# Moving the conditioning loads to GpSimd's queue and the last GpSimd subtractions to VectorE in a two-layer encoder kernel

## The chip, the cores and the metric

The kernel runs on one core of one Trainium2 chip. The metric is the device time of one execution in microseconds. A measurement is the median over runs; the profile is one further execution of the same program, taken by the hardware profiler.

The engines are named as the profile names them: PE is TensorE (PEld its weight load), DVE is VectorE, ACT is ScalarE, POOL is GpSimd and SP is SyncE. A name with a q behind it (ACTq, POOLq, SPq) is the instruction queue of that engine where it issues a DMA or waits.

## The reference, cut to what matters

Two layers work on x of 256 tokens by 1024 features. Six vectors per layer come from a conditioning input c.

```python
cond = jax.nn.silu(c)
for l in range(DEPTH):
    ada = cond @ w_ada[l] + b_ada[l]
    sh1, sc1, g1, sh2, sc2, g2 = jnp.split(ada, 6)
    u = x * (1.0 + sc1) + sh1
    mix = hybrid_mixer(u, ...)
    x = layer_norm(ALPHA * x + g1 * mix, ln_g[l, 0], ln_b[l, 0])
    u = x * (1.0 + sc2) + sh2
    ffn = peer_ffn(u, peer_wq[l], peer_keys[l], peer_u[l], peer_v[l])
    x = layer_norm(ALPHA * x + g2 * ffn, ln_g[l, 1], ln_b[l, 1])
```

`hybrid_mixer` holds two attentions, a long convolution, three gates and an output product. `peer_ffn` makes queries, picks experts by two rounds of top 16, and multiplies with all 16384 rows of `peer_u` and of `peer_v`.

## The kernel before, in words

**Products in split precision.** Every large product is made of three matmuls in a 32-bit matmul format: a weight tile (128 partitions by 1024 elements) is split into a high part, which ACT writes (line 86), and a low part, raw minus high, which DVE or POOL writes (line 88). The activations have a high and a low part too: `uh` and `ul` hold u transposed. PE then adds high by high, high by low and low by high.

**The weight stream.** `Stream` loads the weight tiles one after the other on SP's queue (line 67) into three raw buffers, and splits up to two tiles ahead of the product that wants them. A flag per tile says whether DVE ("v") or POOL ("g") writes its low part. POOL has the first eight tiles of layer 0, the query tiles and the first 24 tiles of `peer_u` of each layer.

**Order of work.** The order is written out by hand. Each engine runs its own instructions in the order in which the program lists them, and waits for the others by semaphores. Small work is put between the products by generators that are advanced one step at a time (`Background.pump`).

**The conditioning.** `w_ada` comes as 160 tiles of 128 by 512 (and eight larger ones in `start`). `ada` (line 395) takes one tile per call: `ada_load` (line 385) issues loads up to three tiles ahead into three buffers (tag `adaw`), so the load of a tile waits until DVE has used the tile three before it. DVE then multiplies by one column of `cond` and accumulates (lines 416 and 418). After eight tiles four columns are made by PE and DVE. 48 tiles go beside layer 0's mixer, 96 beside layer 0's products with `peer_v` (lines 1543 to 1552), and 16 beside layer 1's.

**A part of u^T.** `u_part` (line 465) makes two of the eight 128 by 128 blocks of one token half: PE transposes x (line 475), ACT writes the two high blocks with scale and bias (line 478), ACT or DVE writes the full values into `uft` (lines 481 and 483), and the engine named by `sub` writes the low part (line 486).

**The crossing.** `cross` (line 987) leads from one block to the next and is met three times: from layer 0's mixer to its experts, from there to layer 1's mixer, and from that mixer to its experts. Token half 0 is normalised first. Its four parts of u^T are made, and only then are the two `norm_part` calls of half 1 listed (line 1007); each has three DVE operations of 512 elements (lines 495, 496 and 498). Then `norm_end(1)` has a chain of small DVE operations from line 504 and two of line 520 that write x. PE meanwhile has half 0's first products with the early tiles (line 1018) and then waits for half 1's x.

**Early tiles.** The first four weight tiles behind a crossing are loaded and split ahead of it (`early_split`, line 1058): ACT writes the high part (line 1064), POOL the low part (line 1065). In a mixer this happens beside the output product (line 1217), at the end of the experts beside the last pairs (line 1563). Two raw buffers serve the four tiles.

**Other work of POOL.** It scales x by rows of the layer norm between the products (`scale_x`, line 527), issues the loads of layer 1's constants (`self.loader` is POOL from line 1569 on, until the end of the experts), and clears two tiles.

Of the kernel before, what the change touches and what calls it, by code (L numbers as in the profile page):

```python
# [9 lines left out]
F32 = mybir.dt.float32  # L10
# [5 lines left out]
ALU = mybir.AluOpType  # L16
# [140 lines left out]
class Trunk:  # L157
# [104 lines left out]
    def start(self):  # L262


        nc, a, st = self.nc, self.a, self.st
        with self.tc.tile_pool(name="su", bufs=5) as su:
            tiles = []

            def load():
                t = su.tile([128, 4, 512], F32, tag="su", name="su")  # L270
                nc.sync.dma_start(out=t, in_=a["wada0"][len(tiles)])
                tiles.append(t)

            def sums(kp):
                acc = [self.wk.tile([128, 512], F32, tag="wk", name="acc0") for _ in range(2)]
                for kk in range(8):
                    t, w = acc[kk % 2], tiles[2 * kp + kk // 4][:, kk % 4, :]
                    if kk < 2:
                        nc.vector.tensor_scalar(out=t, in0=w, scalar1=self.cond[:, kk:kk + 1], scalar2=None,
                                                op0=ALU.mult)  # L280
                    else:
                        nc.vector.scalar_tensor_tensor(out=t, in0=w, scalar=self.cond[:, kk:kk + 1], in1=t,
                                                       op0=ALU.mult, op1=ALU.add)
                return acc

            def columns(kp, acc):
                q = self.bp((128, 4, 128))
                for m in range(4):
                    for i in range(2):
                        nc.tensor.matmul(q[:, m, :], acc[i][:, m * 128:m * 128 + 128], self.ident,  # L290
                                         start=(i == 0), stop=(i == 1))
                p = self.sm.tile([128, 2, 2], F32, tag="ac0", name="ac0")
                nc.vector.tensor_reduce(out=p.rearrange("p j k -> p (j k)"), in_=q, op=ALU.add, axis=AX.X)
                ks = slice(2 * kp, 2 * kp + 2)
                nc.vector.tensor_tensor(out=self.adac[:, 0, 0:2, ks], in0=p, in1=self.bcol[:, 0, 0:2, ks], op=ALU.add)

            def load_x(kp):
                s = slice(kp * 256, kp * 256 + 256)
                nc.sync.dma_start(out=self.x[:, :, s], in_=a["x"].rearrange("(p T) d -> p T d", T=2)[:, :, s])

            load()
            load()
            load_x(0)
            st._load()
            for kp in range(1, 4):
                load_x(kp)
                load()
            pairs = {n: self.pair() for n in (5, 4)}
            loads = self.layer_loads(0)
            st.run(3)  # L310
            acc = sums(0)

            def products(n, kp):
                self.tok_mm(pairs[n], self.uh, self.ul, st.get(("tok", 0, n, kp)), 2 * kp, 2, 8)
                self.bg.pump()
                next(loads, None)

            for kp in range(4):
                columns(kp, acc)
                for T in range(2):  # L320
                    self.u_part(T, 2 * kp, "va"[T], "vg"[T])
                if kp < 3:
                    acc = sums(kp + 1)
                for _ in range((2, 1, 0, 0)[kp]):
                    load()
                if kp:
                    products(4, kp - 1)
                self.bg.pump()
                products(5, kp)
            products(4, 3)  # L330
        return pairs
# [53 lines left out]
    def ada_load(self):  # L385

        while self.ada_next < min(self.ada_pos + 3, len(self.ada_todo)):
            i = self.ada_next
            l, j, k, h = self.ada_todo[i]
            t = self.sm.tile([128, 512], F32, tag="adaw", name="adaw", bufs=3)  # L390
            self.ada_tiles[i] = t
            self.nc.scalar.dma_start(out=t, in_=self.a["wada"][l, j, k, h])
            self.ada_next += 1

    def ada(self, until, most=1000):
# [66 lines left out]
            sc, sh = a2, b2  # L462
        self.ucol = sc, sh

    def u_part(self, T, k, scale="v", sub="v"):


        nc = self.nc
        sc, sh = self.ucol
        ts = slice(T * 128, T * 128 + 128)  # L470
        p = self.bp((128, 2, 128))
        t = self.wk.tile([128, 2, 128], F32, tag="wk", name="uft")
        hi, lo = self.uh[:, k:k + 2, ts], self.ul[:, k:k + 2, ts]
        for i in range(2):
            nc.tensor.transpose(p[:, i, :], self.x[:, T, (k + i) * 128:(k + i) * 128 + 128], self.ident)
        cols = [(sc[:, k + i:k + i + 1], sh[:, k + i:k + i + 1]) for i in range(2)]
        for i, (a, b) in enumerate(cols):
            nc.scalar.activation(out=hi[:, i, :], in_=p[:, i, :], func=AF.Identity, scale=a, bias=b)
        for i, (a, b) in enumerate(cols):
            if scale == "a":  # L480
                nc.scalar.activation(out=t[:, i, :], in_=p[:, i, :], func=AF.Identity, scale=a, bias=b)
            else:
                nc.vector.tensor_scalar(out=t[:, i, :], in0=p[:, i, :], scalar1=a, scalar2=b,
                                        op0=ALU.mult, op1=ALU.add)
        eng = nc.gpsimd if sub == "g" else nc.vector
        eng.tensor_tensor(out=lo, in0=t, in1=hi.bitcast(F32), op=ALU.subtract)

    def norm_part(self, T, h, acc):

# [497 lines left out]
    def cross(self, sums, tail):  # L987

        st = self.st
        self.norm_part(0, 1, sums[0][1])
        self.norm_end(0)
        n = len(tail) * 4 // 5
        for mm in tail[:n]:
            mm()
        c = self.wk.tile([128, 512], F32, tag="wk", name="c11")
        self.nc.scalar.activation(out=c, in_=sums[1][1], func=AF.Copy)
        self.u_part(0, 0, "a", "g")
        self.u_part(0, 2, "a", "g")  # L1000
        self.u_part(0, 4, "a", "g")
        self.u_part(0, 6, "a", "g")
        for mm in tail[n:]:
            mm()
        st.release()
        for h in (1, 0):
            self.norm_part(1, h, c if h else sums[1][h])
        ps = [self.pair()[0], self.pair()[0]]
        tiles = self.early_parts

        def products(T, kp):

            ts = slice(T * 128, T * 128 + 128)
            todo = [(self.uh, kp, part) for part in range(2)] + [(self.ul, i, 0) for i in (kp - 1, kp) if 0 <= i and (i < kp or kp == 3)]
            for x, i, part in todo:
                w = tiles[i][part].rearrange("p (k n) -> p k n", k=2)
                for kk in range(2):
                    self.nc.tensor.matmul(ps[T], x[:, 2 * i + kk, ts], w[:, kk, :],
                                          start=x is self.uh and i + kk + part == 0, stop=x is self.ul and i + kk == 4)

        products(0, 0)
        products(0, 1)
        self.norm_end(1)
        st.run(2)
        products(0, 2)
        products(0, 3)
        self.u_part(1, 0, "v", "v")
        self.u_part(1, 2, "a", "g")
        products(1, 0)
        self.u_part(1, 4, "v", "v")  # L1030
        products(1, 1)
        self.u_part(1, 6, "a", "g")
        done = [self.wk.tile([128, 512], F32, tag="wk", name="cr") for _ in range(2)]
        self.nc.scalar.activation(out=done[0], in_=ps[0], func=AF.Copy)
        st.run()
        products(1, 2)
        products(1, 3)
        self.nc.scalar.activation(out=done[1], in_=ps[1], func=AF.Copy)
        self.ext.close()
        st.own = None  # L1040
        return done
# [16 lines left out]
    def early_split(self):  # L1058

        if self.early_raw:  # L1060
            t = self.early_raw.pop(0)
            n = len(self.early_parts)
            h, w = (self.st.own.tile([128, 1024], F32R, name=f"e{i}{n}") for i in range(2))
            self.nc.scalar.activation(out=h, in_=t, func=AF.Copy)  # L1064
            self.nc.gpsimd.tensor_tensor(out=w, in0=t, in1=h.bitcast(F32), op=ALU.subtract)  # L1065
            self.early_parts.append((h, w))
            self.early_load()

# [635 lines left out]
```

## Time and profile before

| | |
|---|---|
| runs | 2396.04, 2402.9, 2398.36 us; median 2398.36 us |
| profiled execution | 2398.13 us, of which the span from the first to the last instruction is 2396.1 us |
| mean granted clock of PE | 0.982 of full speed |
| PE busy | 2274.4 us (95%) |
| DVE busy | 1812.5 us (76%) |
| ACT busy | 1169.6 us (49%) |
| POOL busy | 325.0 us (14%) |

The busy time of an engine is counted from its instructions. Matmuls are pipelined and overlap one another in the rows, so that a busy PE is not a PE at its peak. Two levels of the granted clock occur, 0.5 (1.2 GHz) and 1.0 (2.4 GHz); a mean in between is a mixture.

### The profile page before, as it was taken

To read this page: it belongs to the slowest core of one execution; us is meant where nothing else is said; L and a number is where in the kernel's file an instruction comes from. 1 tells how busy PE (TensorE), PEld (TensorE's weight loads), DVE (VectorE), ACT (ScalarE), POOL (GpSimd) and SP (SyncE) were. 2 spreads that over 40 slices of the span, in tenths; PEclk is the share of its full clock that TensorE was granted. 3 is DMA by queue.
4 is the path that set the end of the run, shared out by engine and by line. 5 is a ranking of instruction groups with operands and counts; after the bars stand their busy time and mean duration, and the time that the engine had idled before them with its cause. 6 is when DMAs were issued, how large, how long until landed. Compare 5 with 4: busy or idle time off the path is not lost.

```text
span 2396.1 us, 38147 instructions
## 1 busy us (share of the span) xinstructions
PE 2274.4 (95%) x14400; PEld 2005.1 (84%) x14400; DVE 1812.5 (76%) x3418; ACT 1169.6 (49%) x1860; POOL 325.0 (14%) x181
## 2 busy tenths in 40 slices
PE   6999989989999999999999999998999999999997
PEld 4688767889999988886777987798999999888786
DVE  6896897977788867778886858879577886755656
ACT  3544444635555444445455454454455554444443
POOL 3100004660000000003023000358100000000200
PEclk9999999999999999999999999999999999999999
DMA  7553664445555568888655434454455555766664
GB/s 289 179 164 97 193 201 145 147 141 168 166 161 167 168 227 267 267 271 278 212 198 176 135 102 141 158 167 145 152 166 165 167 166 179 244 195 193 208 206 149
DMA packets 132592, 438.43 MB, mean 183 GB/s; under 512 B 16370, under 2 KB 17742, under 8 KB 130361
## 3 DMA queue, kind: packets, MB, share of 16 engines
q1 hardware_dynamic: 103328, 377.01, 49.2%
q10 hardware_dynamic: 26968, 51.23, 6.1%
q0 software_dynamic: 2112, 7.77, 1.1%
q8 instruction: 113, 1.85, 0.3%
q14 instruction: 71, 0.57, 0.1%
HBM read 432.80 MB, written 3.15 MB: 182 GB/s over the span
## 4 chain that ended last, share of the span: by engine, by line
PE 69%; DVE 22%; ACT 3%; DMA 3%; issue 3%; ACTq 0%; POOL 0%; DVEq 0%; POOLq 0%
PE bg L209 26%; PE pj L1550 25%; PE pj L197 8%; DVE lo L88 4%; ACT hi L86 1%; DVE eq L1322 1%; DMA raw<-in_v 1%; PE gp L1449 1%; PE gp L1450 1%; PE pj L209 1%; PE bg L662 1%; DVE eq L1317 1%; DVE x L1254 1%; DVE acc L418 1%; DVE sc L1250 1%
## 5 line engine op out<-in xcount | busy, mean ns | idle before, releaser
L88 DVE TENSOR_TENSOR lo<-raw,hi 128x1024 fp32r<-128x1024 f32 x610 | 755.6, 1241 | 330.1 <-ACT hi L86 322.0
L86 ACT ACTIVATE hi<-raw 128x1024 fp32r<-128x1024 f32 x688 | 726.1, 1057 | 443.9 <-PE pj L1550 264.8
L209 PE MATMUL bg<-uh,hi 128*128 128x256 f32 x2240 | 644.7, 288 | 5.9 <-ACT hi L86 5.9
L209 PE MATMUL bg<-uh,lo 128*128 128x256 f32 x2240 | 637.5, 285 | 8.5 <-POOL lo L88 8.5
L1550 PE MATMUL pj<-hi,P 128*128 128x512 f32 x2048 | 637.6, 392 | 6.0 <-DVE P L1495 2.1
L209 PE MATMUL bg<-ul,hi 128*128 128x256 f32 x2240 | 636.6, 284 | 0.0
L1550 PEld LDWEIGHTS pj<-hi,P 128*128 128x128 f32 x2048 | 384.1, 189 | 91.7 <-ACT hi L86 5.0
L209 PEld LDWEIGHTS bg<-uh,lo 128*128 128x128 f32 x2240 | 432.7, 193 | 10.2 <-POOL lo L88 10.2
L209 PEld LDWEIGHTS bg<-uh,hi 128*128 128x128 f32 x2240 | 433.1, 193 | 6.4 <-ACT hi L86 6.3
L209 PEld LDWEIGHTS bg<-ul,hi 128*128 128x128 f32 x2240 | 433.0, 193 | 0.1
L1550 PE MATMUL pj<-lo,P 128*128 128x512 f32 x1024 | 401.3, 392 | 6.8 <-DVE lo L88 6.8
L1550 PEld LDWEIGHTS pj<-lo,P 128*128 128x128 f32 x1024 | 192.9, 188 | 51.3 <-DVE lo L88 11.2
L88 POOL TENSOR_TENSOR lo<-raw,hi 128x1024 fp32r<-128x1024 f32 x78 | 205.6, 2653 | 101.0 <-ACT hi L86 95.6
L1479 ACT ACTIVATE bg<-bg 128x256 f32<-128x256 f32 (+24 forms) x208 | 56.8, 273 | 290.7 <-PE bg L209 290.7
L197 PE MATMUL pj<-hi,uh 128*128 128x512 f32 x432 | 188.8, 437 | 4.7 <-DVE mt L1175 2.3
L197 PE MATMUL pj<-hi,ul 128*128 128x512 f32 x432 | 174.6, 404 | 7.5 <-DVE ul L1235 6.2
L197 PE MATMUL pj<-lo,uh 128*128 128x512 f32 x432 | 174.0, 403 | 7.2 <-DVE lo L88 7.2
L183 POOL DMA_DIRECT2D x<-spill x2 | 1.3, 652 | 1109.8 <-DVE P L1495 1109.8
L1456 DVE SCALAR_TENSOR_TENSOR b<-gp,b 128x160 f32<-128x160 f32 (+6 forms) x236 | 58.8, 310 | 103.5 <-ACT b L1454 103.5
L1065 POOL TENSOR_TENSOR e<-early,e 128x1024 fp32r<-128x1024 f32 x12 | 31.4, 2614 | 621.2 <-ACT e L1064 333.2
L197 PEld LDWEIGHTS pj<-hi,uh 128*128 128x128 f32 x432 | 84.2, 195 | 30.5 <-issue 7.4
L418 DVE SCALAR_TENSOR_TENSOR acc<-adaw,cond,acc 128x512 f32<-128x512 f32 x140 | 109.5, 782 | 0.0
(317 smaller groups left out, 2881.8 us busy)
## 6 DMA issues: line engine op xcount, KB each, us to landing
raw<-in_u SPq DMA_DIRECT2D x256, 512.0 KB, 3.5
raw<-in_v SPq DMA_DIRECT2D x256, 512.0 KB, 4.2
raw<-in_wtok SPq DMA_DIRECT2D x92, 512.0 KB, 3.7
adaw<-in_wada ACTq DMA_DIRECT2D x160, 256.0 KB, 4.0
raw<-in_whyd SPq DMA_DIRECT2D x24, 512.0 KB, 3.6
raw<-in_wq SPq DMA_DIRECT2D x24, 512.0 KB, 3.6
raw<-in_wbr SPq DMA_DIRECT2D x20, 512.0 KB, 3.6
su<-in_wada SPq DMA_DIRECT2D x8, 1024.0 KB, 10.1
```

Of the source, the lines that this page charges most:

```text
L86: self.nc.scalar.activation(out=h, in_=t, func=AF.Copy)
L88: eng.tensor_tensor(out=w, in0=t, in1=h.bitcast(F32), op=ALU.subtract)
L197: self.nc.tensor.matmul(psums[T], l[:, k, s], m[:, kk, :], start=(k == 0 and j == 0), stop=(k == K - 1 and j == 2))
L209: self.nc.tensor.matmul(ps, m[:, k, :], x[:, k, :], start=(k == 0 and j == 0), stop=(k == 7 and j == 2))
L418: nc.vector.scalar_tensor_tensor(out=acc, in0=w, scalar=self.cond[:, k:k + 1], in1=acc, op0=ALU.mult, op1=ALU.add)
L662: nc.tensor.matmul(ps[P], self.fwd[:, P, c, :], z[:, P, :], start=True, stop=True)
L1065: self.nc.gpsimd.tensor_tensor(out=w, in0=t, in1=h.bitcast(F32), op=ALU.subtract)
L1250: nc.vector.match_replace(out=s, in_to_replace=v[:, 0:8], in_values=s, imm_value=LOWEST)
L1254: nc.vector.max_index(out=i[:, 8:16], in_max=v[:, 8:16], in_values=s)
L1456: nc.vector.scalar_tensor_tensor(out=t[:, :, ts], in0=pr[:, i:j, :], scalar=1.0 / GATE_UNIT, in1=t[:, :, ts], op0=ALU.mult, op1=ALU.mult)
L1479: nc.scalar.activation(out=p[:, 0:n], in_=p[:, 0:n], func=AF.Gelu)
L1550: self.nc.tensor.matmul(self.vacc[T][h], x[:, s], v[:, w], start=start and c == 0, stop=stop and c == 2)
```

## The change

The loads of the conditioning tiles go out on POOL's queue instead of ACT's. The low parts of u^T, 22 of the 32 of which POOL wrote, and the low parts of the 12 early tiles are all written by DVE. The argument `sub` is gone. The order in which the program lists its steps is the same.

```diff
@@ start
                 for T in range(2):
-                    self.u_part(T, 2 * kp, "va"[T], "vg"[T])
+                    self.u_part(T, 2 * kp, "va"[T])
@@ ada_load
             self.ada_tiles[i] = t
-            self.nc.scalar.dma_start(out=t, in_=self.a["wada"][l, j, k, h])
+            self.nc.gpsimd.dma_start(out=t, in_=self.a["wada"][l, j, k, h])
             self.ada_next += 1
@@ u_part
-    def u_part(self, T, k, scale="v", sub="v"):
+    def u_part(self, T, k, scale="v"):
...
-        eng = nc.gpsimd if sub == "g" else nc.vector
-        eng.tensor_tensor(out=lo, in0=t, in1=hi.bitcast(F32), op=ALU.subtract)
+        nc.vector.tensor_tensor(out=lo, in0=t, in1=hi.bitcast(F32), op=ALU.subtract)
@@ cross
-        self.u_part(0, 0, "a", "g")
-        self.u_part(0, 2, "a", "g")
-        self.u_part(0, 4, "a", "g")
-        self.u_part(0, 6, "a", "g")
+        self.u_part(0, 0, "a")
+        self.u_part(0, 2, "a")
+        self.u_part(0, 4, "a")
+        self.u_part(0, 6, "a")
...
-        self.u_part(1, 0, "v", "v")
-        self.u_part(1, 2, "a", "g")
+        self.u_part(1, 0, "v")
+        self.u_part(1, 2, "a")
         products(1, 0)
-        self.u_part(1, 4, "v", "v")
+        self.u_part(1, 4, "v")
         products(1, 1)
-        self.u_part(1, 6, "a", "g")
+        self.u_part(1, 6, "a")
@@ early_split
             self.nc.scalar.activation(out=h, in_=t, func=AF.Copy)
-            self.nc.gpsimd.tensor_tensor(out=w, in0=t, in1=h.bitcast(F32), op=ALU.subtract)
+            self.nc.vector.tensor_tensor(out=w, in0=t, in1=h.bitcast(F32), op=ALU.subtract)
```

## Rows read from the trace of the kernel before

**Rows 1.** Stretches of 60 us: length, busy us by engine, PE clock, DMA share, GB/s.

```profile
300.00:360.00 60.00, 50.07 (x236) 39.93 (x236) 55.12 (x70) 24.77 (x32) 2.40 (x1) 0.94 0.63 204
...
900.00:960.00 60.00, 60.00 (x271) 49.69 (x270) 46.45 (x55) 28.31 (x34) 0.00 (x0) 1.00 0.82 270
...
1080.00:1140.00 60.00, 54.81 (x218) 39.78 (x217) 48.55 (x60) 29.77 (x35) 24.73 (x27) 0.97 0.82 271
```

**Rows 2.** Groups of instructions on POOL: count, then busy us, mean ns, idle before.

```profile
L1065 POOL TENSOR_TENSOR e<-early,e 128x1024 fp32r<-128x1024 f32 x12 | 31.4, 2614 | 621.2 <-ACT e L1064 333.2 <-DMA raw<-in_wout 288.1
L486 POOL TENSOR_TENSOR ul<-uft,uh 128x256 fp32r<-128x256 f32 x22 | 17.1, 778 | 61.2 <-ACT uft L481 58.1 <-DMA raw<-in_wtok 3.1
...
L532 POOL DMA_DIRECT2D lnrow<-in_ln x6 | 3.4, 568 | 0.9 <-POOL x L539 0.9
```

**Rows 3.** The page's costliest group of DVE, the low parts of the weight tiles.

```profile
L88 DVE TENSOR_TENSOR lo<-raw,hi 128x1024 fp32r<-128x1024 f32 x610 | 755.6, 1241 | 330.1 <-ACT hi L86 322.0
```

**Rows 4.** Line 486's instructions on DVE: ns minimum, median, maximum.

```profile
L486 DVE TENSOR_TENSOR ul<-uft,uh x10: 424/426/870, 21.3 to 1563.6; 128x256 fp32r<-128x256 f32 x10
```

**Rows 5.** The tile `adaw`: who issues and reads it, and its landing.

```profile
L392 ACTq DMA_DIRECT2D adaw<-in_wada x160: 333/334/690, 70.8 to 2072.4; - x160
L418 DVE SCALAR_TENSOR_TENSOR acc<-adaw,cond,acc x140: 733/746/2858, 77.3 to 2079.8; 128x512 f32<-128x512 f32 x140
...
DMA to landing us min/median/max: 2.5/4.0/9.0
```

**Rows 6.** DMA issues: KB each, median us from issue to landing.

```profile
ld<-in_log_decay POOLq DMA_DIRECT2D x2, 512.0 KB, 9.1
```

**Rows 7.** Second crossing, instructions by time: start, us, engine, line [idle before].

```profile
1251.63 0.69 DVE L495 TENSOR_TENSOR nt<-c,gbc 128x512 f32<-128x512 f32 x1
...
1253.08 0.69 DVE L498 BATCH_NORM_STATS2 stats<-x 128x6 f32<-128x512 f32 x1
...
1256.67 0.89 ACT L481 ACTIVATE uft<-bg,b,a 128x128 f32<-128x128 f32 x2
1256.88 0.21 DVE L504 BATCH_NORM_AGGREGATE mv<-stats 128x2 f32<-128x12 f32 x1
...
1259.43 1.00 DVE L520 TENSOR_SCALAR x<-x,mv,rs 128x512 f32<-128x512 f32 x2
1260.03 0.66 PE L475 MATMUL bg<-ident,x 128*128 128x128 f32 x4 [0.70 <-DVE x L520]
```

**Rows 8.** First crossing, instructions by time.

```profile
385.71 0.89 ACT L481 ACTIVATE uft<-bg,b,a 128x128 f32<-128x128 f32 x2
...
387.63 4.90 POOL L88 TENSOR_TENSOR lo<-raw,hi 128x1024 fp32r<-128x1024 f32 x2 [0.21 <-ACT hi L86]
...
389.07 3.74 DVE L520 TENSOR_SCALAR x<-x,mv,rs 128x512 f32<-128x512 f32 x2
...
390.36 0.66 PE L475 MATMUL bg<-ident,x 128*128 128x128 f32 x4 [0.69 <-DVE x L520]
```

**Rows 9.** Third crossing, instructions by time.

```profile
1552.20 0.89 ACT L481 ACTIVATE uft<-bg,b,a 128x128 f32<-128x128 f32 x2
...
1559.42 0.66 PE L475 MATMUL bg<-ident,x 128*128 128x128 f32 x4 [1.70 <-DVE x L520]
```

**Rows 10.** Output product of layer 0, instructions by time.

```profile
356.13 2.86 DVE L418 SCALAR_TENSOR_TENSOR acc<-adaw,cond,acc 128x512 f32<-128x512 f32 x1
...
365.35 0.80 PE L197 MATMUL pj<-hi,ul 128*128 128x512 f32 x1 [3.13 <-DVE ul L1235]
```

**Rows 11.** End of layer 0's experts, instructions by time.

```profile
1237.48 2.55 DVE L1495 TENSOR_TENSOR P<-b,P 128x512 fp32r<-128x512 f32 x1 [0.24 <-ACT P L1494]
...
1240.08 0.49 PE L1550 MATMUL pj<-hi,P 128*128 128x512 f32 x1 [1.13 <-DVE P L1495]
```

**Rows 12.** Stretches of 2 us, columns as in Rows 1.

```profile
512.00:514.00 2.00, 2.00 (x12) 2.00 (x11) 0.85 (x2) 2.00 (x7) 0.00 (x0) 0.51 0.08 31
...
1242.00:1244.00 2.00, 2.00 (x7) 1.48 (x6) 0.97 (x2) 0.00 (x0) 0.37 (x1) 0.50 0.72 248
```

## The prediction, made before the changed kernel was seen

> **What bounds the kernel now.** I read the stretches of 60 us first, then the waits of PE, then the groups of POOL and the tile `adaw`, and last the instructions by time around each place that the change touches. The stretches [rows 1] show a PE that is busy all the time where nothing else goes on (900 to 960 us), and one that loses 10 us of 60 where DVE is busy for 55 (300 to 360 us). PE sets the pace, and its holes come from DVE and from the hand-overs. ACT, which the change relieves, is half idle in all three stretches. So a microsecond counts only where DVE or a hand-over is what PE waits for: the start, the output products, the end of the experts and the three crossings.
>
> A second thing to see is that POOL is not a free helper. While POOL subtracts a tile, DVE operations that read two operands from the same memory stand still: the accumulation at 356.13 us took 2.86 us [rows 10] against a median of 0.746 [rows 5], and the preparation at 1237.48 took 2.55 [rows 11] against 0.69 for another DVE operation of 512 elements [rows 7].
>
> **The loads.** ACT loses 160 issues at 0.334 us [rows 5], 53 us, and its waits for a free buffer. POOL gets 160 issues; its own cost 0.568 us [rows 2], so 91 us on an engine with 325 us of work. What ACT gives up is mostly slack, since PE's large holes trace back to DVE. Bounds are a gain of 2 us, if ACT's waits reach PE somewhere, and a loss of 2 us, if the first load of a group comes late; I take 0.5 us of gain, nearer to nothing because ACT is half idle [rows 1].
>
> On POOL's queue the loads wait for DVE's accumulation, and behind them stand the scaling of x and the loads of layer 1's constants, which before ran ahead of the program. Nothing of that is wanted within the next tile, except the row loads of the filters, which took 9.1 us to land [rows 6]. Tied to the loads, the scaling is spread over more tiles, and DVE stands still for it in smaller portions. In that stretch PE was busy for 54.81 of 60 us [rows 1]. The bounds are that all 5 us come back, or that 3 us more are lost to a late row load; I take a gain of 1.5.
>
> Of POOL's issue the Trainium skill says in "SBUF — State Buffer", section "SBUF: two separate sides", that GpSimd writes the descriptors of its DMAs itself and cannot while VectorE runs an operation that takes both ports; a DMA of 620 ns alone became one of 3100 ns there. No row of this case shows it: POOL's issues took 0.568 us on average [rows 2]. By that rule an estimate of the landing is 4.0 + 2.5 us, which three buffers still cover; it only makes the third rival likelier.
>
> **The early tiles.** Twelve POOL operations of 2614 ns [rows 2] become twelve DVE operations of 1241 ns [rows 3]. Before, each could hold DVE for 2.86 less 0.75, 2.1 us. In layer 0's output product two of them lie in front of the last low part that PE waits 3.13 us for [rows 10], so it comes 2 x (2.1 - 1.2) = 1.8 us earlier: gain 1.8. If PE's clock no longer falls there another 3 us could come; I don't count them, because most of the wait stays. In layer 1 the later tiles' raw data arrives late, and DVE now waits for it where POOL did; that costs what the missing hold gives: 0.4 us lost. At the end of the experts DVE is free at 1237.48 - 0.24 = 1237.24; its own tile and the preparation take 1.24 + 0.69, so the latter ends at 1239.2 instead of 1240.03. That takes 0.9 off PE's wait of 1.13 [rows 11], and with the hole go some 2 us at half clock behind it [rows 12], worth 1.0: gain 1.9.
>
> **The start.** Four small subtractions go to DVE, the bound there: 4 x 0.424 [rows 4] = 1.7 us, less what POOL's 0.778 [rows 2] held DVE up, about 0.3 each. Loss 0.5.
>
> **The crossings** decide. Before, POOL took each low part of half 0 when ACT was done, and DVE meanwhile ran the two `norm_part` calls of half 1. Now these calls stand behind four subtractions on DVE's queue, and the last of those must wait for ACT's last `uft`. What follows on DVE is two times 2.14 us (1251.63 to the end of 1253.08 [rows 7]), then 2.55 us of small operations (1256.88 to 1259.43), then 0.6 us until PE begins to transpose (1260.03).
>
> Second crossing: ACT ends at 1256.67 + 0.89 = 1257.56. One subtraction and its wait, 0.5, gives 1258.05; 4.3 more 1262.35; 2.55 more 1264.9; 0.6 more 1265.5. PE began at 1260.03 [rows 7]: loss 5.5.
> First crossing: 385.71 + 0.89 + 0.5 + 4.3 + 2.55 + 0.6 = 394.55 against 390.36 [rows 8]: loss 4.2. It is less because line 520 was itself held by POOL's tiles (3.74 instead of 1.00), which are over by then.
> Third crossing: 1552.20 + 0.89 + 0.5 + 4.3 + 2.55 + 0.6 = 1561.04 against 1559.42 [rows 9]: loss 1.6, and 0.4 from the output product before it.
> The waits of PE grow from 0.70 to about 6 us in the second and from 0.69 to about 5 in the first. After a hole of that length in another stage PE ran at 0.51 of its clock [rows 12], for some 4 us. That costs 2 us where PE is the bound; here ACT paces part of it, so I take 1.5 each, with 0 and 2 as bounds. The six subtractions of half 1 cost nothing: DVE's 0.424 is shorter than POOL's 0.778, and their readers come later.
>
> **Sum.** -0.5 - 1.5 - 1.8 + 0.4 - 1.9 + 0.5 + 5.5 + 4.2 + 1.6 + 3.0 = +9.5 us. On the profiled execution's own 2398.13 us this gives 2407.6 us; that execution lies 0.2 us below the median of the runs. A difference of 0.3%, 7.2 us, is about what a measurement of this kernel can tell from no change, so the forecast is slower, by 0.4%.
>
> **Rivals.**
> *Gains and losses meet.* The crossings lose 11.3 us but no clock, the scaling gives all 5 us back, the output product gets its 3 us of clock, ACT's relief is worth 2: 11.3 + 0.4 + 0.5 - 2 - 5 - 4.8 - 1.9 = -1.5, 2396.6 us. For it speaks that the fall of the clock depends on what PE did shortly before; against it, that every bound would have to fall on one side.
> *POOL was the brake (faster).* One mechanism: POOL's tile operations hold DVE, and without them the DVE-bound stages speed up. Twelve holds of 2.1 less 1.24 us are 10 us; with 5 from the scaling, 5 from clock that no longer falls and 2 from ACT it is 22 against the 11.3 us of the crossings: 2387. It decides if most holds lie on PE's path; against it, a single hold was seen in front of PE at the end of the experts and two in layer 0's output product.
> *Late loads.* If POOL's loads land as late as its slowest, 9.1 us [rows 6], three buffers allow one tile per (9.1 + 0.57 + 0.75)/3 = 3.5 us. PE takes a tile of 12 matmuls in 60 x 12/271 = 2.66 us [rows 1]. Eight tiles then take 27.8 us where ten tile times, two of them without a load, are 26.6: 1.2 us lost per group, 14 us over the 12 groups of layer 0's experts: 2421. Against it: the loads are smaller, and landed in 4.0 us [rows 5].
>
> **How the numbers follow.** The forecast gets 0.45, the first rival 0.35, the second 0.12, the third 0.08. Slower is 0.45 + 0.08 = 0.53, the same 0.35, faster 0.12. The range of 2394 to 2419 runs from just below the first rival to the sum with every unknown at its dear bound (2 instead of -0.5, 3 instead of -1.5, clock 4 instead of 3, and 3 more of clock in the third crossing); it leaves out the second and third rival, 0.2.
>
> **What would show it.** In each crossing DVE's line 495 of half 1 starts behind the fourth line 486, and PE's line 475 after a wait of 5 to 6 us in the first two and some 3 us in the third, with half clock behind it. In layer 0's output product line 418 falls back to 0.75 us and PE's last wait to about 2.5. The tile `adaw` lands within 6 us and DVE never waits for it. Wrong would be: transposes no later than before, loads that DVE waits for, or a lasting gain in the stretch at 1080 us of more than 5 us.

## The result and the profile after

The changed kernel took 2421.78 us (median of four runs, 2418.97 to 2422.38) against 2397.2 us of the kernel before in the same measurement: a ratio of 1.0098, with a 95% interval of 1.0076 to 1.0120. It is slower by about 24 us, and the interval lies clear of no change. The forecast was slower by 9.5 us, at 2407.6 us; the direction was right, the size was not, and the time lies beyond the upper end of the range of 2394 to 2419. One execution of the version with the loads alone (below) took 3712 us at a mean granted clock of 0.557; it is in that version's median (2402.16 us; 2401.87 without it) and not in its ratio.

The profiled execution has a span of 2419.8 us (2396.1 before) and a mean granted clock of 0.979 (0.982). The first section of its page shows engines as busy as before; POOL alone has more to do:

```profile
PE 2278.4 (94%) x14400; PEld 2009.1 (83%) x14400; DVE 1815.0 (75%) x3452; ACT 1168.8 (48%) x1860; POOL 362.2 (15%) x307
```

So the loss is waiting. The list of PE's waits (us in total, times, the longest) names the place: the transposes waited 5.4 us in the whole kernel before (first line), and now 24.0, most of it in the crossings.

```profile
PE bg L475 <- DVE x L520: 5.4, 5, 2.1
...
PE bg L474 <- DVE x L518: 24.0, 5, 7.6
...
PE bg L602 <- DMA w<-in_hy_w: 3.6, 2, 2.6
```

PE's instructions come in the same order in both kernels, so the two traces can be laid beside each other. Lines behind 484 have moved up by two: 474 is the 475 of before, 484 the 486, 494 the 496, 518 the 520. The table takes one instruction at the end of each stretch and says how much later it starts, beyond what had gathered before it.

| stretch, up to | before | after | forecast | lost |
|---|---|---|---|---|
| last `uft` of half 0, first crossing | 385.71 | 382.62 | -1.3 | -3.1 |
| first line 209 behind the first crossing | 398.19 | 402.58 | +5.7 | +7.5 |
| a high part (line 86) ahead of layer 1's loads | 1081.31 | 1085.36 | 0 | -0.3 |
| the copy `c` at the end of layer 0's experts | 1249.41 | 1257.52 | -3.9 | +4.1 |
| first line 197 behind the second crossing | 1267.90 | 1282.49 | +7.0 | +6.5 |
| last `uft` of half 0, third crossing | 1552.20 | 1569.03 | +0.4 | +2.2 |
| first line 209 behind the third crossing | 1566.62 | 1589.65 | +1.6 | +6.2 |
| end of the span | 2396.1 | 2419.8 | 0 | +0.7 |
| sum | | | +9.5 | +23.7 |

(A row's loss is the difference of the two delays, rounded.) Three stretches carry the gap of 14 us: layer 0's products with `peer_v` with the end of the experts (8 us), the third crossing (4.6) and the first (1.8). The second crossing came out as forecast.

Two rows are no safe ground. Up to that last `uft` five of the versions below run the same program as the changed kernel, and their traces reach it between 2.6 us earlier and 1.5 us later than the kernel before; the changed kernel's was 3.1 earlier. From the second crossing to the third, the kernel before with the query tiles on DVE (the last version below) has nothing changed, and its trace lost 2.8 us. So the gain of 3.1 and the loss of 2.2 can be the difference between two executions.

**The third crossing.** Instructions by time (start, us, engine, line, idle before and what ended it):

```profile
1569.03 0.89 ACT L480 ACTIVATE uft<-bg,b,a 128x128 f32<-128x128 f32 x2
...
1569.95 0.43 DVE L484 TENSOR_TENSOR ul<-uft,uh 128x256 fp32r<-128x256 f32 x1 [0.97 <-ACT uft L480]
1570.29 0.69 DVE L493 TENSOR_TENSOR nt<-c,gbc 128x512 f32<-128x512 f32 x1
1571.08 2.81 DVE L494 SCALAR_TENSOR_TENSOR x<-x,nt 128x512 f32<-128x512 f32 x1
...
1574.53 0.67 DVE L493 TENSOR_TENSOR nt<-pj,gbc 128x512 f32<-128x512 f32 x1
1575.24 1.40 DVE L494 SCALAR_TENSOR_TENSOR x<-x,nt 128x512 f32<-128x512 f32 x1
...
1579.95 1.00 DVE L518 TENSOR_SCALAR x<-x,mv,rs 128x512 f32<-128x512 f32 x2
...
1570.94 5.15 POOL L88 TENSOR_TENSOR lo<-raw,hi 128x1024 fp32r<-128x1024 f32 x2 [44.01 <-ACT hi L86]
...
1580.55 1.12 PE L474 MATMUL bg<-ident,x 128*128 128x128 f32 x4 [7.57 <-DVE x L518]
```

The order is the one forecast: `norm_part` of half 1 (line 493) starts behind the fourth subtraction, and that behind ACT's last `uft`. But a second thing happens in it. POOL splits its two query tiles from 1570.94 on, and line 494 takes 2.81 and 1.40 us where 0.69 is its usual time: 2.8 us more. The transposes start 4.3 us late (21.13 less the 16.83 gathered), which is the forecast's 1.6 and these 2.8. The first crossing shows the same:

```profile
384.53 5.14 POOL L88 TENSOR_TENSOR lo<-raw,hi 128x1024 fp32r<-128x1024 f32 x2 [11.83 <-ACT hi L86]
...
384.60 2.87 DVE L494 SCALAR_TENSOR_TENSOR x<-x,nt 128x512 f32<-128x512 f32 x1
...
388.82 1.40 DVE L494 SCALAR_TENSOR_TENSOR x<-x,nt 128x512 f32<-128x512 f32 x1
...
394.13 1.12 PE L474 MATMUL bg<-ident,x 128*128 128x128 f32 x4 [7.54 <-DVE x L518]
```

In the second crossing DVE itself splits the next tiles, behind line 518, and line 494 keeps its 0.69 us. Its transposes start 13.39 - 8.1 = 5.3 us late, where 5.5 was forecast:

```profile
1266.77 0.69 DVE L494 SCALAR_TENSOR_TENSOR x<-x,nt 128x512 f32<-128x512 f32 x1
...
1273.42 1.11 PE L474 MATMUL bg<-ident,x 128*128 128x128 f32 x4 [5.95 <-DVE x L518]
```

Which operations POOL holds is regular. The Trainium skill says in "SBUF — State Buffer", section "SBUF: two separate sides", that VectorE and GpSimd share one pair of ports as an exclusive lock, which VectorE needs for an operation with two inputs from SBUF or in a two-port mode, and that whoever starts first keeps it for the whole instruction. The trace agrees: line 493 with one input from PSUM (`pj`) ran in 0.67 us in the middle of POOL's 5.15 us, line 494 with two from SBUF did not.

Behind each hole the clock fell to its lower level, as the stretches of 2 us show (behind the length stands PE busy; PEclk is the number ahead of the DMA share). In the kernel before it was 1.00 at these places in all three crossings; the first line shows its third, the others are of the changed kernel:

```profile
1560.00:1562.00 2.00, 1.67 (x8) 1.22 (x8) 1.15 (x3) 2.00 (x7) 0.00 (x0) 1.00 0.77 254
...
394.00:396.00 2.00, 1.75 (x6) 1.29 (x7) 0.77 (x3) 1.14 (x4) 0.00 (x0) 0.50 0.00 0
...
1274.00:1276.00 2.00, 1.88 (x6) 1.32 (x5) 2.00 (x2) 1.85 (x6) 0.00 (x0) 0.50 0.18 12
...
1508.00:1510.00 2.00, 2.00 (x6) 1.54 (x5) 1.97 (x3) 0.00 (x0) 0.00 (x0) 0.50 0.82 242
...
1580.00:1582.00 2.00, 1.33 (x5) 0.93 (x5) 0.95 (x2) 0.72 (x3) 0.00 (x0) 0.50 0.00 0
...
1722.00:1724.00 2.00, 1.57 (x16) 1.57 (x16) 0.38 (x1) 0.00 (x0) 0.00 (x0) 0.55 0.35 137
```

The stretches at 1508 and 1722 us lie far from the change. They hold some of the loss in layer 1's mixer and of the last row of the table; that the change caused these two is not shown.

**The products with `peer_v`.** Here the loads matter. POOL, ACT and PE by time, after:

```profile
1118.92 0.58 POOL L392 DMA_DIRECT2D adaw<-in_wada  x1 [4.52 <-DVE acc L418]
1119.49 0.53 POOL L530 DMA_DIRECT2D lnrow<-in_ln  x1
1120.02 0.53 POOL L183 DMA_DIRECT2D w<-in_hy_w  x1
1120.53 1.08 POOL L183 DMA_DIRECT2D ld<-in_log_decay  x2
...
1133.42 2.09 PE L602 MATMUL bg<-w,h 64*128 64x512 f32 x4 [2.61 <-DMA w<-in_hy_w]
...
1137.76 1.28 ACT L594 ACT_TABLE_LOAD   x1 [5.08 <-DMA ld<-in_log_decay]
```

and before:

```profile
1098.89 0.58 POOL L532 DMA_DIRECT2D lnrow<-in_ln  x1 [0.30 <-POOL x L539]
1099.47 0.53 POOL L183 DMA_DIRECT2D w<-in_hy_w  x1
1099.98 1.09 POOL L183 DMA_DIRECT2D ld<-in_log_decay  x2
```

The same three loads went out 20.5 us later, while the work around them was 4 us late at most: ahead of them stood conditioning loads that waited for DVE, and the scaling tied to those. When they landed, PE had waited 2.61 us for the filter's weight and ACT 5.08 for the rows, with PE's next high parts behind it on ACT's queue. Up to 1111.21 us of the kernel before, there had been a gain: that high part came at 1108.45, so the shift had gone from +4.1 to -2.8. The scaling in portions may have brought it. But in the kernel before the rows were landing there, and ACT waited for a raw tile, where the changed kernel had not issued the rows yet:

```profile
1111.21 1.06 ACT L86 ACTIVATE hi<-raw 128x1024 fp32r<-128x1024 f32 x1 [5.55 <-DMA raw<-in_v]
```

So part of the gain may be only the same transfers, put off. At ACT's next step with the rows (1123.59, now 1139.05) the shift was +15.5.

The rows were also longer on their way. From issue to landing they took (least, median, most; the least is layer 0's load) before and after

```profile
DMA to landing us min/median/max: 7.2/7.9/10.3
...
DMA to landing us min/median/max: 7.4/15.3/16.6
```

The conditioning tiles themselves did well in the main (issues, use on DVE, and landing). DVE waited for none by the trace; the one that took 17.0 us stood behind the rows:

```profile
L392 POOL DMA_DIRECT2D adaw<-in_wada x160: 536/536/736, 66.9 to 2097.3; - x160
L418 DVE SCALAR_TENSOR_TENSOR acc<-adaw,cond,acc x140: 736/745/751, 77.2 to 2104.4; 128x512 f32<-128x512 f32 x140
...
DMA to landing us min/median/max: 2.7/4.0/17.0
```

**What was gained.** DVE's accumulation is never held any more (751 ns at most, 2858 before [rows 5]). In layer 0's output product PE's wait for low parts fell from 5.6 us (2.48 and 3.13 [rows 10]) to

```profile
PE pj L197 <- DVE ul L1233: 2.4, 2, 1.7
```

But other waits came in: from 310 to 380 us all of PE's waits add up to 13.0 us in both traces. At the end of the experts PE no longer waits for line 1493; its 1.13 us [rows 11] are gone, and only this is left:

```profile
PE pj L1548 <- DVE lo L88: 0.8, 2, 0.6
PE pj L1548 <- ACT hi L86: 0.2, 1, 0.2
```

### The profile page after: what moved, and what is told of

Read it like the earlier page. It is cut to its first block, busy times and chain, and to the rows that moved or that the text cites. A ratio compares the mean times of both kernels' runs of the same rounds, so it can differ in the third digit from the quotient of the medians.

```text
span 2419.8 us, 38133 instructions
## 1 busy us (share of the span) xinstructions
PE 2278.4 (94%) x14400; PEld 2009.1 (83%) x14400; DVE 1815.0 (75%) x3452; ACT 1168.8 (48%) x1860; POOL 362.2 (15%) x307
## 4 chain that ended last, share of the span: by engine, by line
PE 67%; DVE 23%; ACT 4%; DMA 4%; issue 3%; ACTq 0%; POOL 0%; DVEq 0%; POOLq 0%
PE bg L209 26%; PE pj L1548 24%; PE pj L197 7%; DVE lo L88 4%; ACT hi L86 1%; DVE eq L1320 1%; PE gp L1447 1%; PE gp L1448 1%; PE pj L209 1%; PE bg L660 1%; DMA raw<-in_v 1%; PE pj L1016 1%; DVE acc L418 1%; DVE eq L1315 1%; DVE x L1252 1%
## 5 line engine op out<-in xcount | busy, mean ns | idle before, releaser
L392 POOL DMA_DIRECT2D adaw<-in_wada x160 | 86.4, 540 | 1255.5 <-DVE acc L416 871.9
L197 PEld LDWEIGHTS pj<-lo,uh 128*128 128x128 f32 x432 | 83.2, 193 | 27.3 <-DVE lo L88 9.9
L418 DVE SCALAR_TENSOR_TENSOR acc<-adaw,cond,acc 128x512 f32<-128x512 f32 x140 | 104.3, 745 | 0.0
```

Of the source, the lines that this page charges most:

```text
L197: self.nc.tensor.matmul(psums[T], l[:, k, s], m[:, kk, :], start=(k == 0 and j == 0), stop=(k == K - 1 and j == 2))
L392: self.nc.gpsimd.dma_start(out=t, in_=self.a["wada"][l, j, k, h])
L418: nc.vector.scalar_tensor_tensor(out=acc, in0=w, scalar=self.cond[:, k:k + 1], in1=acc, op0=ALU.mult, op1=ALU.add)
```

## The experiments

Each version was timed against the kernel before on the same chip; the ratio (with its 95% interval) is the safer number, since the median of before moved between 2397.2 and 2398.7 us from one measurement to the next. It is not the quotient of the two medians, and can differ from that by up to 0.1%.

### The change in three parts

**The loads alone** (kernel before, `ada_load` on POOL):

```diff
-            self.nc.scalar.dma_start(out=t, in_=self.a["wada"][l, j, k, h])
+            self.nc.gpsimd.dma_start(out=t, in_=self.a["wada"][l, j, k, h])
```

> The kernel before with one part of the change: the conditioning loads on POOL's queue. Queue theory: in layer 0's products with peer_v the loads of layer 1's filter rows stand on POOL's queue behind conditioning loads that wait for DVE, land some 15 us late, ACT waits for them in front of the next high parts and PE runs dry; the changed kernel lost 5.9 us between 1081 and 1190 us that way, so this kernel should take 2397.2 + 6 = 2403 us (2400 to 2406), and the wait of ACT for the rows should be seen again. Rival (the prediction's term): the scaling spread over more tiles gives 1.5 us and ACT's relief 0.5, 2395 us, and the loss in that stretch of the changed kernel came from the subtractions on DVE.

Measured: 2402.16 us, 1.0017 (1.0007 to 1.0028). The loads cost some 4 us by themselves; the gain of 2 us of the prediction is excluded. In the list of ACT's waits the rows of layer 1 stand with 6.6 us (in the kernel before there is no wait for them):

```profile
ACT L596 <- DMA ld<-in_log_decay: 6.6, 1, 6.6
```

**The early tiles alone** (kernel before, `early_split` on DVE):

```diff
-            self.nc.gpsimd.tensor_tensor(out=w, in0=t, in1=h.bitcast(F32), op=ALU.subtract)
+            self.nc.vector.tensor_tensor(out=w, in0=t, in1=h.bitcast(F32), op=ALU.subtract)
```

> The kernel before with one part of the change: the low parts of the 12 early tiles on DVE. Hold theory: DVE was held longer by POOL's subtraction than its own takes; the changed kernel gained 3.0 us up to the end of layer 0's output product and 1.9 at the end of its experts, and lost perhaps 0.7 in layer 1's output product: 2397.2 - 4.2 = 2393 us (2391 to 2395). Rival: POOL's work was free cover and DVE is the bound there, 12 x 1.24 us of which a third lies on the path: 2402 us.

Measured: 2397.08 us, 1.0006 (0.9994 to 1.0017). Both theories missed. The profiled execution alone had gained 4 us (span 2392.1), but at a granted clock of 0.984, and five of the twelve runs lie above 2401 us. That the early tiles shorten the kernel is not shown.

**Half 0's low parts alone** (kernel before, four calls in `cross`):

```diff
-        self.u_part(0, 0, "a", "g")
+        self.u_part(0, 0, "a", "v")
...
```

> The kernel before with one part of the change: in the three crossings the four low parts of token half 0 are written by DVE. Order and hold theory: the norm of half 1 stands behind the last of them, and in the first and third crossing POOL's two query tiles then hold it for another 2.8 us; the changed kernel lost 7.7, 6.9 and 5.9 us in the three, 20.5 in sum: 2417.7 us (2414 to 2420). Rival (the prediction's terms): 5.5 + 4.2 + 1.6 and 3.0 of clock: 2411.5 us.

Measured: 2418.81 us, 1.0082 (1.0066 to 1.0097), with these waits of the transposes:

```profile
PE bg L475 <- DVE x L520: 21.1, 3, 7.6
```

This part carries 20 of the 24 us, and the prediction's terms for it (14.3) lie below the interval (15.8 to 23.3 us). The three parts together give 0.17 + 0.06 + 0.82 = 1.05%, the whole change 0.98%. Within the intervals nothing is left for the ten small subtractions of the start and of half 1, which no part holds.

### Why the crossings cost so much

**The same work in another order** (changed kernel; `u_part` keeps its subtraction back in `later`):

```diff
+        self.norm_part(1, 1, c)
+        later = []
+        for k in (0, 2, 4, 6):
+            self.u_part(0, k, "a", later)
-        self.u_part(0, 0, "a")
...
         st.release()
-        for h in (1, 0):
-            self.norm_part(1, h, c if h else sums[1][h])
+        later.pop(0)()
+        later.pop(0)()
+        self.norm_part(1, 0, sums[1][0])
+        later.pop(0)()
+        later.pop(0)()
```

> The changed kernel, with DVE's work in the crossings listed in another order: the norm of half 1's first 512 columns ahead of the four low parts of half 0, that of the other 512 columns between the second and the third. The same instructions run on the same engines. Order theory: PE's transposes of half 1 come only some 0.8 to 1.2 us later than in the kernel before, not 7.1, 5.3 and 4.3; with the clock behind them that gives 6.9 + 5.7 + 5.1 = 17.7 us back: 2421.8 - 17.7 = 2404 us (2401 to 2407). Rival: DVE simply has 12 operations of 0.43 us more in front of the transposes wherever they are listed, and the rest is clock or POOL's holds: at most 3 to 4 us back, 2418 us.

Measured: 2399.69 us, 1.0006 (0.9993 to 1.0019): 22 us less with the same 3452 instructions on DVE. The transposes of half 1 in the three crossings (PE by time):

```profile
391.89 0.66 PE L474 MATMUL bg<-ident,x 128*128 128x128 f32 x4 [0.68 <-DVE x L522]
...
1263.11 0.66 PE L474 MATMUL bg<-ident,x 128*128 128x128 f32 x4 [1.75 <-DVE x L522]
...
1562.80 0.66 PE L474 MATMUL bg<-ident,x 128*128 128x128 f32 x4 [0.67 <-DVE x L522]
```

The work of 0.43 us per subtraction was never the price; the place was. It gave back more than the 17.7 us expected, in part because the last of these waits is even shorter than in the kernel before (1.70 [rows 9]). By the stretches of the table the three crossings lost -0.2, 1.0 and -2.2 us here; the trace of the loads alone, where the crossings are those of before, has -2.0 in the third as well.

**POOL's hold taken away** (changed kernel; the query tiles 4 and 5, which POOL splits in the first and third crossing, go to DVE):

```diff
-                st.add(("wq", l, i), a["wq"][l, i], "v" if i == 6 else "g")
+                st.add(("wq", l, i), a["wq"][l, i], "v" if i < 7 else "g")
```

> The changed kernel, with the low parts of the first two query tiles behind the first and third crossing written by DVE instead of POOL (in the second crossing they already are DVE's). Hold theory: line 494 falls back from 2.8 and 1.4 us to 0.69 each, the transposes come 2.9 and 2.6 us earlier, and DVE's own two subtractions stand behind line 518 where ACT is waited for anyway: 2421.8 - 5.5 = 2416.3 us (2414 to 2419). Rival: POOL's subtraction was harmless cover, and DVE has 4 x 1.24 us more on the path: 2421.8 + 0 to 5 us.

Measured: 2416.09 us, 1.0078 (1.0057 to 1.0100), where 2416.3 was expected. In the first crossing line 494 is back at 0.69 us, and the transposes wait 7.5 us less in sum than in the changed kernel:

```profile
387.69 0.69 DVE L494 SCALAR_TENSOR_TENSOR x<-x,nt 128x512 f32<-128x512 f32 x1
...
389.73 0.69 DVE L494 SCALAR_TENSOR_TENSOR x<-x,nt 128x512 f32<-128x512 f32 x1
```

```profile
PE bg L474 <- DVE x L518: 16.5, 5, 6.0
```

The times alone do not settle it, since the interval touches that of the changed kernel; the rows do.

### Why the loads cost instead of paying

**x's and layer 1's constants on ACT's queue** (changed kernel, in the products with `peer_v`):

```diff
-                    self.loader = nc.gpsimd
+                    self.loader = nc.scalar
```

> The changed kernel, with the loads of layer 1's constants (and of x) on ACT's queue instead of POOL's, so that they no longer stand behind the conditioning loads; the row loads of the scaling stay on POOL. Queue theory: the loss of 5.9 us in the products with peer_v goes, and some of the gain that the changed kernel had reached before the rows were late (up to 6.9 us against before) stays: 2421.8 - 5.9 = 2416 us, down to 2411. Rival (POOL's loads land late whatever stands ahead of them, or the conditioning loads themselves are too slow): no change, 2421 to 2423 us.

Measured: 2417.82 us, 1.0085 (1.0071 to 1.0100), 4 us less where 5.9 had been expected, and the interval overlaps that of the changed kernel. The traces say it more sharply. From the high part at 1081.31 us of the kernel before to the one at 1191.2 (the same two instructions in each trace), the changed kernel lost 6.0 us and the loads alone 7.4; here it is 0.3. The four versions in which all these loads go out as before lie between -0.5 and 0.4 there.

**The late loads issued early, still on POOL's queue** (kernel before with `ada_load` on POOL):

```diff
             ld = fp.tile([128, 2048], F32, name="ld")
+            if l:
+                self.load(w3, a["hy_w3"][l])
+                for i in range(0, 2048, 1024):
+                    self.load(ld[:, i:i + 1024], a["log_decay"][l][i:i + 1024].partition_broadcast(128))
...
-            self.load(w3, a["hy_w3"][l])
...
```

> The kernel before with the conditioning loads on POOL's queue, as in the run of that part alone (2402.2 us), and with the filter's late loads of layer 1 (the third weight and the rows of the decay, 1 MB) issued together with the filter's first loads, ahead of the scaling and of the conditioning loads that wait. Queue theory: neither PE nor ACT waits for them, the 6 to 7 us that this stretch lost go, and a little of the gain from the scaling in portions stays: 2395.5 us (2393 to 2398). Rival: it is the transfer of the rows beside the weight stream that costs, or the scaling's new places, and not where they stand in the queue: 2400 to 2403 us.

Measured: 2405.29 us, 1.0020 (1.0005 to 1.0036): a miss, and the theory as I had put it fell. The trace shows what happened (POOL, PE and DVE by time):

```profile
1093.35 0.57 POOL L183 DMA_DIRECT2D ld<-in_log_decay  x1 [7.98 <-DMA x<-spill]
...
1094.91 1.08 PE L574 MATMUL bg<-hh,w 33*64 33x256 f32 x2 [4.02 <-DMA w<-in_hy_w]
...
1104.97 0.75 DVE L418 SCALAR_TENSOR_TENSOR acc<-adaw,cond,acc 128x512 f32<-128x512 f32 x1 [6.31 <-DMA adaw<-in_wada]
...
1110.93 0.54 PE L1554 MATMUL pj<-lo,P 128*128 128x512 f32 x1 [3.72 <-DVE lo L88]
```

Now it is the load of the rows that waits on POOL's queue, until x has landed, and the conditioning loads stand behind it. They land late, DVE waits 6.31 us for one, and the low part behind that wait is late for PE. Between the same two instructions 8.0 us were lost.

The rows do not need x. In none of the fourteen traces does a load on POOL's queue go out before the eighth load ahead of it there has landed; counted from x's, the first load of the rows is the eighth here. In the changed kernel the added conditioning load makes the scaling's first row load the eighth: it waited 5.45 us for x, and in the kernel before, as the seventh, not at all.

The rival, that the rows' transfer costs and not their place, is not ruled out by this run. PE's longest single wait here is the 4.02 us for the filter's first weight, which landed 12.7 us after its issue (8.7 in the loads alone) while the DMA engines were 93 to 98% busy (1080 to 1100 us). That is a crowd of transfers as much as a place in the queue.

**The two kinds on two queues** (kernel before, `ada_load` on POOL, and the loader on ACT's queue as above):

```diff
-            self.nc.scalar.dma_start(out=t, in_=self.a["wada"][l, j, k, h])
+            self.nc.gpsimd.dma_start(out=t, in_=self.a["wada"][l, j, k, h])
...
-                    self.loader = nc.gpsimd
+                    self.loader = nc.scalar
```

> The kernel before with the conditioning loads on POOL's queue (that part alone took 2402.2 us), and with x's and layer 1's constants loaded on ACT's queue, so that only the scaling and its row loads share POOL's queue with the conditioning. Queue theory, after the early rows failed: what costs is that a load on POOL's queue stands behind another instruction there that waits, whichever of the two it is; with the constants off the queue the 4 to 6 us of that stretch go: 2397.5 us (2395 to 2400). Rival: what costs is the rows' transfer or the scaling in its new places, and the queue has no part in it: 2401 to 2404 us.

Measured: 2399.06 us, 1.0001 (0.9989 to 1.0014): 3 us less than the loads alone, level with the kernel before. The stretch lost 1.0 us instead of 7.4, and ACT's wait for the rows falls from 6.6 us to 3.2, for their two halves:

```profile
ACT L596 <- DMA ld<-in_log_decay: 2.1, 1, 2.1
...
ACT ld L596 <- DMA ld<-in_log_decay: 1.1, 1, 1.1
```

But the second queue does not give the rows their lead back. On ACT's queue they go out behind a high part that waits for its raw tile, later still than on POOL's. Times are counted from the high part at 1081.31 us of the kernel before:

| version | first half of the rows goes out | lands after | lost up to 1191.2 |
|---|---|---|---|
| kernel before | 18.7 | 7.9 | 0 |
| changed kernel | 35.2 | 15.3 | 6.0 |
| the loads alone | 34.7 | 15.7 | 7.4 |
| changed kernel, constants on ACT's queue | 38.8 | 8.0 | 0.3 |
| this version | 39.0 | 8.0 | 1.0 |

What separates the cheap versions from the dear ones is the landing and not the issue. In the changed kernel five loads left POOL's queue within 2.1 us (1119.49 to 1121.61), behind a conditioning load that had waited for DVE, and they landed one after the other from 1129.4 to 1138.7. On two queues the filter's weight left 6 us ahead of the rows. Whether the order in the queue or the crowd of transfers made the landing long, no run separates.

### Putting it together

**All three repairs** (changed kernel with the new order, the query tiles on DVE and the early rows):

```diff
+        self.norm_part(1, 1, c)
...
+                st.add(("wq", l, i), a["wq"][l, i], "v" if i < 7 else "g")
...
+            if l:
+                self.load(w3, a["hy_w3"][l])
...
```

> The changed kernel with all three repairs: the new order on DVE in the crossings, the first query tiles' low parts on DVE, and the filter's late loads issued early. Theory: 17.7 us from the order, 5 to 7 from the loads, and 0 to 2 from the query tiles, whose holds stand on line 518 in this order: 2421.8 - 24 = 2398 us (2394 to 2401), level with the kernel before. Rival: if the repairs' gains overlap or the clock does not come back, 2405 to 2410 us.

Measured: 2398.90 us, 1.0004 (0.9992 to 1.0015). The time was met, its parts were not: the order alone had already given that much, and the early rows give nothing (the stretch up to 1191.2 us lost 6.3 us, against 4.6 with the order alone).

**The new order, and the constants on ACT's queue** (changed kernel):

```diff
+        self.norm_part(1, 1, c)
...
-                    self.loader = nc.gpsimd
+                    self.loader = nc.scalar
```

> The changed kernel with the new order on DVE in the crossings (alone 2399.7 us) and x's and layer 1's constants on ACT's queue. Queue theory: again 4 to 5.5 us less, 2395 us (2393 to 2397), below the kernel before. Rival: 2400 us, and the loads have no part left once the crossings are repaired.

Measured: 2396.27 us, 0.9986 (0.9973 to 0.9998), 3.4 us less than the order alone. It is the third pair in which the second queue gives 3 to 4 us. The intervals overlap in each pair; the traces are clearer, with 4.6 us lost up to 1191.2 us by the order alone and 1.6 here.

**The new order, the conditioning loads back on ACT, the query tiles on DVE** (changed kernel):

```diff
-            self.nc.gpsimd.dma_start(out=t, in_=self.a["wada"][l, j, k, h])
+            self.nc.scalar.dma_start(out=t, in_=self.a["wada"][l, j, k, h])
...
+        self.norm_part(1, 1, c)
...
+                st.add(("wq", l, i), a["wq"][l, i], "v" if i < 7 else "g")
```

> A version meant to beat both: the changed kernel with the new order on DVE in the crossings, the conditioning loads back on ACT's queue, and the first two query tiles behind the first and third crossing on DVE. Theory: the crossings then cost 0.3 us against before and give up to 2.6 us of PE's waits back with the holds on the last lines 518, the early tiles give 0 to 3: 2394.5 us (2391 to 2397). Rival: each of these is hidden anyway, 2398 us.

Measured: 2394.08 us, 0.9979 (0.9967 to 0.9991), 5 us less than the kernel before and 28 less than the changed one: the fastest version found, though the gain over before is smaller than 0.3%. Its transposes wait as long as before:

```profile
PE bg L474 <- DVE x L522: 5.4, 5, 1.8
```

**The query tiles on DVE in the kernel before:**

```diff
-                st.add(("wq", l, i), a["wq"][l, i], "v" if i == 6 else "g")
+                st.add(("wq", l, i), a["wq"][l, i], "v" if i < 7 else "g")
```

> The kernel before with one step: the low parts of the first two query tiles behind the first and third crossing on DVE instead of POOL. Hold theory: line 520 falls from 3.74 and 2.69 us to 1.00 in front of the transposes, of which PE waits for the first of its two halves alone, so about 1 us each is to be had: 2396 us (2394.5 to 2398). Rival: DVE's own 4 x 1.24 us stand on the path: 2400 us.

Measured: 2397.31 us, 0.9991 (0.9977 to 1.0004). This is inconclusive: the expected size, but no change lies within the interval.

## Why the prediction was wrong

- **The loads: the sign was wrong.** The prediction saw that behind the waiting loads "stand the scaling of x and the loads of layer 1's constants, which before ran ahead of the program". It excepted "the row loads of the filters, which took 9.1 us to land", set 3 us as the bound for them, and took a gain of 1.5, with 0.5 more for ACT's relief. Measured by the loads alone: a loss of 4 us, 2 to 7 by the interval. The step that failed is that the rows were given the landing that they had before. Behind the conditioning loads they went out 16.5 us later in the program and took 15.3 and 16.6 us to land, so that ACT waited 5.08 us for them and PE 2.61 for the filter's weight. The late issue alone is not the price: on ACT's queue they went out later still, and the stretch lost 1.6 us at most. Why the landing took so long stays open. The gain of 6.8 us up to 1111 us may be the scaling in portions, as forecast, or the rows' transfer put off.
- **The crossings: the mechanism was right, one term was missing.** The wait behind ACT's last `uft` came as described, and moving the norm ahead of it gave back all that the crossings had cost. The second crossing was met (5.5 forecast, 5.3 measured). In the first the prediction said that POOL's tiles "are over by then" and looked at line 520 alone. POOL began at the same point of the crossing as before and met line 494 instead. That is the missing term: 2.9 us in the first crossing and 2.8 in the third, where the prediction had none of it. Of the 20 us that this part measured alone, the prediction had 14.3.
- **The clock** is put at 0.6, 1.2 and 1.9 us behind the three crossings (what the stretches lost less the delay of the transposes); the 3.0 us forecast for the first two and nothing for the third are about that sum, in other places.
- **The early tiles** shortened the waits that were named, but in the output product others took their place. At the end of the experts (1191.2 us to the copy `c`) the changed kernel gained 1.9 us, as forecast, and seven of the eight traces with these tiles on DVE gained 1.9 to 2.3. But the loads alone, with the tiles on POOL, gained 1.8 too. Alone they gave no change that could be measured. No run shows the 0.4 us set down for layer 1.
- **The start and the six low parts of half 1** were not tested alone; the sum of the parts leaves nothing for them that is clear of the intervals.
- **The third rival** named nearly the right time (2421) by luck: the conditioning loads kept their median landing of 4.0 us, and DVE's accumulations were not what waited. A sign that the prediction had named did fail: seven of the 160 tiles took more than 6 us, one of them 17.0.
- The rule on descriptors that GpSimd cannot write beside VectorE (the Trainium skill, "SBUF — State Buffer", "SBUF: two separate sides") had been weighed in the prediction. The conditioning loads do not bear it out here: with DVE busy for 75% of the time they landed in 4.0 us at the median from either queue. And while the rows were on their way (1120 to 1135 us) the DMA engines did not lie idle, but were 91% busy or more.

Left open: why the rows took so long to land on POOL's queue, and whether the early tiles pay.

## What to carry to other kernels

Before an instruction is moved to another engine's queue, ask what it will wait for there, and follow what stands behind it to its last reader: the price was 0.43 us of work per subtraction and 20 us of waiting, and listing the same instructions in another order gave all of it back. When loads of two kinds are put on one queue, follow each to its landing and not only to its issue: the same rows went out late in seven versions, and the stretch that reads them lost 4.6 to 7.4 us on the shared queue and 0.3 to 1.6 on two. And when work moves away from beside a long operation of another engine, look at what it will run beside instead.

## What the runs showed of the hardware

One and the same kernel spreads over 15 us. Of 35 executions of the kernel before, the fastest took 2392.2 us at a mean granted clock of 0.983 and the slowest 2407.5 us at 0.979; thirteen at 0.983 or more have a median of 2395.9 us, seven at 0.980 or less one of 2402.6 us. A single profile can show a gain of 4 us that twelve runs don't confirm, as with the early tiles.

No load on POOL's queue went out before the eighth load ahead of it there had landed, in any trace: the changed kernel's first row load of the scaling at 1093.79 us, 0.3 us after x had landed, and the rows of the version that issues them early at 1093.35, again 0.3 us after. Between two executions of the same instructions the stretch up to the first crossing differed by 4.6 us (3.1 earlier than before in the changed kernel, 1.5 later with the new order).
